# Wider products, split evictions: the first 56 tiles of the stage of u

## The chip, the cores and the metric

The kernel runs on one core of one Trainium2 chip. The metric is the device time of one execution in microseconds (us); 1671.91 us is the median of 3 runs of the kernel before (1670.87 to 1672.17). Engines are named as the profile names them: PE (TensorE matmuls) with PEld (its weight loads), DVE (VectorE), ACT (ScalarE), POOL (GpSimd) and SP, which only issues transfers here.

## The reference, cut to what matters

The program is three blocks over 256 tokens of width 1024: two attention and MLP layers, one layer with a state-space and an attention branch, and a mixture of 16,384 experts. The change is in the last one:

```python
def peer_ffn(x, w_q, sub_k1, sub_k2, u_tab, v_tab):
    q = x @ w_q                              # 8 heads, two halves of 128
    v1, i1 = top_k(q1 @ sub_k1.T, 16); v2, i2 = top_k(q2 @ sub_k2.T, 16)
    top_s, pos = top_k(v1[:, None] + v2[None, :], 16)
    experts, gates = i1 * 128 + i2 at pos, softmax(top_s)
    u = u_tab[experts]
    act = gelu(sum(u * x)) * gates
    return sum(act * v_tab[experts])
```

The kernel computes, for 224 of the 256 tokens, gelu(u_tab x) for all experts as one dense product (the stage of u), multiplies it by a dense table of gates that is zero for experts not chosen, and multiplies by v_tab (the stage of v). The other 32 tokens gather their rows.

## The kernel before, in words

The kernel is written by hand with a fixed order of instructions on each engine. `peer` starts on line 1537.

**The stage of u.** u_tab comes in 128 tiles of 128 experts, each 128x1024 words (8 blocks of 128x128). A `Weights` object streams them: SP loads a tile into one of four `raw` buffers, ACT copies it to `whi` (line 94, a rounded high part), and DVE or POOL subtracts to get `wlo` (line 96, the low part). There are 3 buffers of each part here, and a call of `take` splits tiles up to two ahead of the one it hands out. While `w.share` is 2 (the takes of tiles 0 to 47) every second split's subtraction goes to POOL: the even tiles of u go to DVE, the odd ones to POOL.

The tokens' side, `hT`, is split too, into `hTl` and `hTh`, two tiles of 128 x 8 x 256. Each tile of u takes 24 products of 224 columns (`mm_cols`, lines 156 and 159): 8 of whi with hTh, 8 of whi with hTl and 8 of wlo with hTh, all into the same 224 columns of a PSUM bank. `u_pair` (line 1762) gives two tiles one bank of the pool `side`, and one activation of 448 columns (line 1772) takes both out of PSUM through Gelu into S0.

**What DVE does beside it.** The routing (top 16 of the keys, then of the candidates, then the choice of indices) is a list of small jobs, `work`. `some` (line 1821) takes jobs up to a budget, and is called twice for each pair. The order on DVE for a pair is then: the subtraction of an even tile, two helpings of jobs, the next even tile's subtraction.

**What sets the order of evictions.** `w.post` keeps a function until the next `take`, which first issues its loads and splits and then flushes what was posted. So what is posted after tile i is issued behind the splits that the take of tile i+1 asks for. Pools hand out banks in rotation; `acc` has 4 and is free in this stage.

From pair U0 = 56 on (and for tiles 64 to 127) `u_pair` stays as it is.

Of the kernel before, what the change touches and what calls it, by code (L numbers as in the profile page):

```python
# [10 lines left out]
FT = mybir.dt.float32  # L11
FR = mybir.dt.float32r
# [3 lines left out]
AF = mybir.ActivationFunctionType  # L16
OP = mybir.AluOpType
AX = mybir.AxisListType

D = 1024  # L20
S = 256
# [7 lines left out]
UT, SE, U0, I0, YN, YA = 32, 19.5, 6, 10, 27.5, 29  # L29
# [108 lines left out]
class Net:  # L138
# [113 lines left out]
                after(hi, lo, pv)  # L252

    def new_T(self, pool, name):
        return tuple(pool.tile([128, 8, S], FR, name=name + x) for x in "hl")


    def sincos(self, ang, out, pool):
# [1274 lines left out]
    def peer(self, ctx, w, hT):  # L1533
        tc, nc, a = self.tc, self.nc, self.a
        V, G = nc.vector, nc.gpsimd
# [5 lines left out]
        N, GR = S - NS, 128 // NS  # L1541
        S0 = sp.tile([128, 64, N], FT, name="S0")
# [4 lines left out]

        eid = sp.tile([128, NS], I32, name="eid")
        eidf, gs, dots = (sp.tile([128, NS], FT, name=n) for n in ("eidf", "gs", "dots"))
        hTd = tuple(x[:, :, 0:N] for x in hT)  # L1550
        late = {}
        it = sp.tile([128, 128], FT, name="it")
        nc.gpsimd.dma_start(out=it, in_=a["iota"])
# [38 lines left out]
        def q_mm(i):  # L1592

            ps = self.acc.tile([128, 512], FT, name="acc")
            for hf in range(2):
                self.mm_cols(ps[:, 256 * hf:256 * hf + 256], w.next(), hT)
            return ps

        def q_T(i):

            w.flush()
            ps = self.bank()
            for hf in range(2):
                for t in range(2):
                    n = 2 * i + hf
                    nc.tensor.transpose(ps[:, 256 * hf + 128 * t:256 * hf + 128 * t + 128], qn[:, t, 128 * n:128 * n + 128],
                                        self.ident)
            return ps
# [91 lines left out]
        def dot_step(n):  # L1700

            fetch(a["un"], n)
            if 2 <= n < NS + 2:
                r = fetched.popleft()
                V.scalar_tensor_tensor(r, r, 1.0, xs, op0=OP.mult, op1=OP.mult, accum_out=dots[:, n - 2:n - 1])  # L1705
            if n == NS + 1:
                nc.scalar.activation(dots, dots, AF.Gelu_apprx_tanh)
                V.tensor_tensor(dots, dots, gs, op=OP.mult)
                late["sum"] = sp.tile([128, D], FT, name="xs")

        def sum_step(n):

            fetch(vn, n)
            if 2 <= n < NS + 2:
                r, y, m = fetched.popleft(), late["sum"], dots[:, n - 2:n - 1]
                if n == 2:
                    V.tensor_scalar(y, r, m, None, op0=OP.mult)
                else:
                    V.scalar_tensor_tensor(y, r, m, y, op0=OP.mult, op1=OP.add)
            if n == NS + 1:  # L1720
                for h in range(2):
                    ps = self.bank()
                    nc.tensor.matmul(ps, late["picks"], late["sum"][:, 512 * h:512 * h + 512], start=True, stop=True)
                    x = late["xr"][128 - NS:128, 1, 512 * h:512 * h + 512]
                    w.post(V.tensor_tensor, x, ps[128 - NS:128], x, op=OP.add)
# [22 lines left out]
        def gate_mm(hf, q):  # L1748
# [9 lines left out]
            if q % 2:  # L1758
                v = (late["S1"] if hf else S0)[:, :, 4 * q - 4:4 * q + 4]
                w.post(lambda: V.tensor_tensor(v, v, ps.rearrange("p (t c) -> p c t", c=64), op=OP.mult))  # L1760

        def u_pair(c, between=None):
            ps = self.bank()
            for x in range(2):
                wt = w.next()
                if x and between:
                    between()
                self.mm_cols(ps[:, 256 * x:256 * x + N], wt, hTd)
            if c == 64:
                late["S1"] = sp.tile([128, 64, N], FT, name="S1")  # L1770
            dst = S0[:, c:c + 2] if c < 64 else late["S1"][:, c - 64:c - 62]
            w.post(lambda: nc.scalar.activation(dst, ps.rearrange("p (a b) -> p a b", a=2)[:, :, 0:N], AF.Gelu_apprx_tanh))  # L1772
# [4 lines left out]
        for n, i in enumerate(order):  # L1777
            ps = q_T(i) if i < 2 else q_mm(i)
# [29 lines left out]
        def some(budget=16):  # L1808
            while work and budget >= work[0][1] // 2:
                f, n = work.popleft()  # L1810
                f()
                budget -= n

        def gate_step(q):

            if q >= 0 and q % 4 == 0:
                for i in range(q, q + 4):
                    gate_mm(i // NQ, i % NQ)
            if q + 4 < 2 * NQ:
                gate_gen((q + 4) // NQ, (q + 4) % NQ)  # L1820

        ops = deque()
        NQ, U0, V0 = N // 4, 56, 52
        for c in range(0, 64, 2):
            w.share = 2 if c < 48 else 0
            if c >= 60:
                gate_step(c - 64)
            u_pair(c, some)
            some()
            if c >= U0:  # L1830
                dot_step((c - U0) // 2)
# [3 lines left out]
        def gate_steps(n, end):  # L1835
            nonlocal q
            for _ in range(n):
                if q < end:
                    gate_step(q)
                    q += 2  # L1840

        def a_split(c, dst=None):
            src = S0[:, c] if c < 64 else late["S1"][:, c - 64]
            A = dst or sp.tile([128, 2 * N], FR, name="ahl", bufs=2)
            ah, al = A[:, 0:N], A[:, N:2 * N]
            nc.scalar.activation(ah, src, AF.Copy)  # L1846
            G.tensor_tensor(al, src, ah.bitcast(FT), op=OP.subtract)  # L1847
            return A

        for c in range(64, 128, 2):  # L1850
            w.share = 6
            if c == 126:
                w.share = 0
                A = []
                u_pair(c, lambda: (gate_steps(1, NQ), A.append(a_split(0))))
                w.flush()
            else:
                u_pair(c, lambda: gate_steps(1, NQ))
            dot_step((c - U0) // 2)
# [7 lines left out]
        acc = [self.acc.tile([128, 512], FT, name="acc") for _ in range(6)]  # L1867
        column = lambda k: acc[k][:, 0:N] if k < 4 else acc[2 + k // 2][:, 256 * (k % 2):256 * (k % 2) + N]

        def v_mm(c, A, wts, ks, last=False):  # L1870

            mm = nc.tensor.matmul
            parts = [(k, i, slice(128 * k, 128 * k + 128)) for k in ks for i in range(len(A))]
            for k, i, s in parts:
                first = c == 0 and i == 0
                if k < 4:
                    mm(acc[k][:, 0:2 * N], wts[i][0][:, s], A[i], start=first, stop=False)  # L1877
                else:
                    mm(column(k), wts[i][0][:, s], A[i][:, 0:N], start=first and k % 2 == 0, stop=False)  # L1879
            for k, i, s in parts:  # L1880
                if k >= 4:
                    mm(column(k), wts[i][0][:, s], A[i][:, N:2 * N], start=False, stop=False)  # L1882
            for k, i, s in parts:
                mm(column(k), wts[i][1][:, s], A[i][:, 0:N], start=False, stop=last and i == len(A) - 1 and (k < 4 or k % 2 == 1))  # L1884

        nxt = A.pop()
        for c in range(124):
            if c == 122:

                w.parts = Room(sp.tile([128, 64 * N], FR, name="S0"))  # L1890
            A = nxt
            wt = w.next()
            nxt = a_split(c + 1)
            v_mm(c, [A], [wt], range(8))
            if c % 2 == (c > 30):
                gate_steps(1, 2 * NQ)
            if c == 8:
                xr = late["xr"] = self.hTp.tile([128, 2, D], FT, name="hTh")
                gb = self.hTp.tile([128, D], FT, name="hTl")
                src = a["norm_f_g"]  # L1900
                nc.scalar.dma_start(out=gb, in_=bass.AP(tensor=src.tensor, offset=src.offset, ap=[[0, 128], [1, D]]))
                for t in range(2):
                    nc.scalar.dma_start(out=xr[:, t], in_=self.xd[t])
                late["picks"] = sp.tile([128, 128], FT, name="it")
                nc.scalar.dma_start(out=late["picks"], in_=a["sums"])
            if c >= V0 and c % 2 == 0:
                sum_step((c - V0) // 2)
# [29 lines left out]
        for b in range(4):  # L1937
# [3 lines left out]
            for i, k in enumerate(ks):  # L1941
                dst = oT[k // 4][:, k % 4]
# [14 lines left out]
        for t in range(2):  # L1957
            for h in range(2):
                c = slice(512 * h, 512 * h + 512)
                x = xr[:, t, c]  # L1960
# [212 lines left out]
```

## Time and profile before

| | before |
|---|---|
| median of 3 runs | 1671.91 us (1670.87 to 1672.17) |
| profiled execution | 1672.08 us, span 1670.0 us |
| PE busy | 1616.1 us (97%), 12410 matmuls |
| DVE busy | 1299.8 us (78%) |
| ACT busy | 845.9 us (51%) |
| POOL busy | 699.0 us (42%) |
| first matmul of the stage of u | 927.16 us into the span |
| first matmul of its tile 56 | 1083.38 us into the span |

The shares of busy time are averages over the whole program; the change touches only the 156 us between the last two rows. A matmul's duration in the profile overlaps with its neighbours, so its cost in a stream is read from the distance between starts.

### The profile page before, as it was taken

What the parts mean: (1) busy time and instruction counts of PE and PEld (TensorE: products, weight loads), DVE (VectorE), ACT (ScalarE), POOL (GpSimd) and SP (SyncE); (2) the same over time, 40 slices, a digit from 0 to 9 for tenths busy, and PEclk for the clock granted to TensorE, in tenths of its full rate; (3) what the DMA queues carried; (4) which work ended last, traced back from release to release, by engine and by line L of the source; (5) the groups of instructions that cost most, each with busy time, mean ns of one, the idle gap of its engine ahead of it and who ended that gap; (6) DMA issues with size and microseconds to landing.
All of it is one profiled execution on the core that took longest, in us unless ns stands there. A gap on an engine that the chain in (4) does not pass through costs nothing.

```text
span 1670.0 us, 31715 instructions
## 1 busy us (share of the span) xinstructions
PE 1616.1 (97%) x12410; PEld 1476.5 (88%) x12410; DVE 1299.8 (78%) x2318; ACT 845.9 (51%) x1308; POOL 699.0 (42%) x610
## 2 busy tenths in 40 slices
PE   8999999889999999997999999999999999999996
PEld 6788999767889998775879999999999999999996
DVE  6775997666769866787663899889999889877775
ACT  6555655455556454643445545544444444455553
POOL 2313529322148933673020454323343222277773
PEclk9999999989999999998999999999999999999998
DMA  7435565464356557823356455777777655689982
GB/s 248 143 122 169 166 188 177 165 205 131 107 187 195 184 162 252 305 77 126 101 171 217 159 177 194 247 228 262 254 258 251 207 178 181 195 291 302 305 301 77
DMA packets 94325, 328.49 MB, mean 197 GB/s; under 512 B 11920, under 2 KB 16176, under 8 KB 93280
## 3 DMA queue, kind: packets, MB, share of 16 engines
q1 hardware_dynamic: 82992, 285.27, 51.1%
q0 software_dynamic: 10176, 39.03, 7.4%
q10 hardware_dynamic: 1008, 2.17, 0.4%
q8 instruction: 97, 1.59, 0.4%
q14 instruction: 52, 0.43, 0.1%
HBM read 318.57 MB, written 7.47 MB: 195 GB/s over the span
## 4 chain that ended last, share of the span: by engine, by line
PE 82%; DVE 8%; ACT 3%; DMA 3%; issue 2%; POOL 1%; ACTq 0%; SPq 0%; POOLq 0%; DVEq 0%
PE side L159 19%; PE acc L159 15%; PE side L156 10%; PE acc L156 8%; PE acc L1884 7%; PE acc L1877 6%; PE acc L1882 3%; PE acc L1879 3%; DVE wlo L96 3%; DMA raw<-in_ws 3%; PE side L1757 2%; ACT whi L94 1%; PE side L399 1%; PE side L376 1%; PE side L375 1%
## 5 line engine op out<-in xcount | busy, mean ns | idle before, releaser
L96 DVE TENSOR_TENSOR wlo<-raw,whi 128x1024 fp32r<-128x1024 f32 x462 | 609.2, 1330 | 221.0 <-ACT whi L94 220.3
L94 ACT ACTIVATE whi<-raw 128x1024 fp32r<-128x1024 f32 x511 | 535.8, 1057 | 456.1 <-PE acc L1882 174.0
L159 PE MATMUL side<-hTh,wlo 128*128 128x224 f32 (+1 forms) x1664 | 224.4, 277 | 2.8 <-DVE wlo L96 2.5
L156 PE MATMUL side<-hTh,whi 128*128 128x224 f32 (+1 forms) x1664 | 225.5, 278 | 0.8 <-ACT Bst L108 0.8
L159 PE MATMUL side<-hTl,whi 128*128 128x224 f32 (+1 forms) x1664 | 223.6, 277 | 0.0
L156 PEld LDWEIGHTS side<-hTh,whi 128*128 128x128 f32 x1664 | 207.6, 191 | 4.0 <-ACT Bst L108 1.1
L159 PEld LDWEIGHTS side<-hTh,wlo 128*128 128x128 f32 x1664 | 205.7, 191 | 3.9 <-DVE wlo L96 3.3
L159 PEld LDWEIGHTS side<-hTl,whi 128*128 128x128 f32 x1664 | 205.9, 191 | 0.0
L96 POOL TENSOR_TENSOR wlo<-raw,whi 128x1024 fp32r<-128x1024 f32 x49 | 125.9, 2572 | 178.2 <-ACT whi L94 170.9
L1847 POOL TENSOR_TENSOR ahl<-S,ahl 128x224 fp32r<-128x224 f32 x125 | 123.4, 988 | 173.8 <-ACT ahl L1846 173.2
L1884 PE MATMUL acc<-ahl,wlo 128*128 128x224 f32 x992 | 130.9, 274 | 0.0
L156 PE MATMUL acc<-whi,hTh 128*128 128x512 f32 x384 | 124.2, 416 | 1.3 <-ACT whi L94 1.3
L1877 PE MATMUL acc<-ahl,whi 128*128 128x448 f32 x496 | 124.4, 372 | 0.7 <-ACT S L1772 0.7
L1884 PEld LDWEIGHTS acc<-ahl,wlo 128*128 128x128 f32 x992 | 120.7, 192 | 0.0
L159 PE MATMUL acc<-wlo,hTh 128*128 128x512 f32 x384 | 117.9, 400 | 1.2 <-DVE wlo L96 1.1
L159 PE MATMUL acc<-whi,hTl 128*128 128x512 f32 x384 | 117.9, 399 | 0.3 <-DVE hTl L222 0.3
L159 PEld LDWEIGHTS acc<-wlo,hTh 128*128 128x128 f32 x384 | 72.7, 190 | 20.7 <-DVE wlo L96 3.2
L797 POOL TENSOR_TENSOR th<-th,cv 128x256 f32<-128x256 f32 x44 | 47.6, 1082 | 103.0 <-DVE th L796 99.6
L783 DVE SCALAR_TENSOR_TENSOR cv<-side,cw,cv 128x254 f32<-128x254 f32 (+1 forms) x176 | 72.5, 472 | 22.3 <-ACT cv L780 22.3
L159 PEld LDWEIGHTS acc<-whi,hTl 128*128 128x128 f32 x384 | 72.9, 190 | 18.3 <-DVE hTl L222 0.8
L1877 PEld LDWEIGHTS acc<-ahl,whi 128*128 128x128 f32 x496 | 84.3, 190 | 5.2 <-issue 1.4
L1696 POOL DMA_INDIRECT rows<-in_un,eid x32 | 47.0, 1470 | 96.4 <-DVE rows L1705 94.3
(487 smaller groups left out, 2787.7 us busy)
## 6 DMA issues: line engine op xcount, KB each, us to landing
raw<-in_ws SPq DMA_DIRECT2D x259, 512.0 KB, 4.0
raw<-in_us SPq DMA_DIRECT2D x128, 512.0 KB, 3.9
raw<-in_vs SPq DMA_DIRECT2D x128, 512.0 KB, 4.2
dBst<-Bst SPq DMA_DIRECT2D x1, 2048.0 KB, 7.4
dCT<-CT SPq DMA_DIRECT2D x2, 1024.0 KB, 7.9
tg<-dBst POOLq DMA_DIRECT2D x1, 2048.0 KB, 9.4
gb<-in_g_ffn SPq DMA_DIRECT2D x2, 512.0 KB, 5.3
s5bc<-in_s5bc SPq DMA_DIRECT2D x2, 512.0 KB, 5.8
```

The costliest lines, as they stand in the source:

```text
L94: self.nc.scalar.activation(hi, t, AF.Copy)
L96: eng.tensor_tensor(lo, t, hi.bitcast(FT), op=OP.subtract)
L156: mm(ps, sh, mh, start=first, stop=False)
L159: mm(ps, sl if side == "s" else sh, ml if side == "m" else mh, start=False, stop=last and side == late)
L783: nc.vector.scalar_tensor_tensor(o[which][:, n:], p[which][:, :S - n], cw[which][:, 2 - n:3 - n], o[which][:, n:], op0=OP.mult, op1=OP.add)
L797: nc.gpsimd.tensor_tensor(th, th, o[1], op=OP.mult)
L1696: G.indirect_dma_start(out=r, out_offset=None, in_=table, in_offset=bass.IndirectOffsetOnAxis(ap=eid[:, n:n + 1], axis=0))
L1847: G.tensor_tensor(al, src, ah.bitcast(FT), op=OP.subtract)
L1877: mm(acc[k][:, 0:2 * N], wts[i][0][:, s], A[i], start=first, stop=False)
L1879: mm(column(k), wts[i][0][:, s], A[i][:, 0:N], start=first and k % 2 == 0, stop=False)
L1882: mm(column(k), wts[i][0][:, s], A[i][:, N:2 * N], start=False, stop=False)
L1884: mm(column(k), wts[i][1][:, s], A[i][:, 0:N], start=False, stop=last and i == len(A) - 1 and (k < 4 or k % 2 == 1))
```

## The change

For pairs below U0 the kernel calls `u_apart` in place of `u_pair`. `hTh` and `hTl` become the two halves of one tile, so that whi is multiplied by both at once: 8 products of 448 columns into columns 0 to 447 of a bank, then 8 of wlo with the high half into columns 0 to 223. Each tile of u has a bank of its own in `acc`. Then ACT copies columns 224 to 447 to S0 (one take later), DVE adds columns 0 to 223 to it (another take later), and after both tiles of a pair ACT applies Gelu in S0 (one more take later).

```diff
     def new_T(self, pool, name):
-        return tuple(pool.tile([128, 8, S], FR, name=name + x) for x in "hl")
+        self.pair = pool.tile([128, 2, 8, S], FR, name=name)
+        return self.pair[:, 0], self.pair[:, 1]
...
-        hTd = tuple(x[:, :, 0:N] for x in hT)
+        hTd = self.pair[:, 0, :, 0:N], self.pair[:, 1, :, 0:N]
...
+        def u_sum(ps, dst):
+            nc.scalar.activation(dst, ps[:, N:2 * N], AF.Copy)
+            w.post(V.tensor_tensor, dst, ps[:, 0:N], dst, op=OP.add)
+
+        def u_apart(c):
+            dst = S0[:, c:c + 2]
+            for x in range(2):
+                wt = w.next()
+                if x:
+                    some()
+                ps = self.acc.tile([128, 512], FT, name="acc")
+                for k in range(8):
+                    nc.tensor.matmul(ps[:, 0:2 * N], wt[0][:, 128 * k:128 * k + 128], self.pair[:, :, k, 0:N], start=k == 0,
+                                     stop=False)
+                for k in range(8):
+                    nc.tensor.matmul(ps[:, 0:N], wt[1][:, 128 * k:128 * k + 128], hTd[0][:, k], start=False, stop=k == 7)
+                w.post(u_sum, ps, dst[:, x])
+            w.post(w.post, w.post, nc.scalar.activation, dst, dst, AF.Gelu_apprx_tanh)
...
-            u_pair(c, some)
+            if c < U0:
+                u_apart(c)
+            else:
+                u_pair(c, some)
```

The rest of the diff reuses the joint tile's room in the stage of v.

On PE, tiles 4 and 5 of u, with the semaphores that an instruction waits for. Before (`side` is the bank of the pair):

```order
L156 MATMUL side<-hTh,whi 128x224 [waits Activation_49]
L156 MATMUL side<-hTh,whi 128x224 x7
L159 MATMUL side<-hTl,whi 128x224 x8
L159 MATMUL side<-hTh,wlo 128x224 [waits DVE_49]
L159 MATMUL side<-hTh,wlo 128x224 x7
L156 MATMUL side<-hTh,whi 128x224 [waits Activation_49]
L156 MATMUL side<-hTh,whi 128x224 x7
L159 MATMUL side<-hTl,whi 128x224 x8
L159 MATMUL side<-hTh,wlo 128x224 [waits Pool_49]
L159 MATMUL side<-hTh,wlo 128x224 x7
```

The same two tiles now, each in a bank of `acc`:

```order
L1777 MATMUL acc<-hT,whi 128x448 [waits DVE_49,Activation_49]
L1777 MATMUL acc<-hT,whi 128x448 x7
L1780 MATMUL acc<-hT,wlo 128x224 x8
L1777 MATMUL acc<-hT,whi 128x448 [waits DVE_49,Activation_49]
L1777 MATMUL acc<-hT,whi 128x448 x7
L1780 MATMUL acc<-hT,wlo 128x224 [waits Pool_49]
L1780 MATMUL acc<-hT,wlo 128x224 x7
```

The wait for DVE has moved from the 17th product of the even tile to its first, and the odd tile's first product has one too.

On DVE, from the subtraction for tile 4 of u to that for tile 6 (L1519 to L1529 are one routing job and the next, MAX and its followers). Before:

```order
L96 TENSOR_TENSOR wlo<-raw,whi 128x1024
L1519 MAX S_9262<-S_9262 128x8 x2
L1521 MAX_INDEX S_9262<-S_9262 128x8 x2
L1523 MATCH_REPLACE S_9262<-S_9262 128x128 x2
L1527 MAX S_9262<-S_9262 128x8 x2
L1529 MAX_INDEX S_9262<-S_9262 128x8 x2
```

The same place now (S_9252 is S0; L108 is where a posted function is called):

```order
L96 TENSOR_TENSOR wlo<-raw,whi 128x1024
L108 TENSOR_TENSOR S_9252<-acc,S_9252 128x224 x2
L1520 MAX S_9253<-S_9253 128x8 x2
L1522 MAX_INDEX S_9253<-S_9253 128x8 x2
L1524 MATCH_REPLACE S_9253<-S_9253 128x128 x2
L1528 MAX S_9253<-S_9253 128x8 x2
L1530 MAX_INDEX S_9253<-S_9253 128x8 x2
```

Two additions stand behind each subtraction for an even tile; the first is that of the tile four before it.

## Rows read from the trace of the kernel before

**Rows 1.** Windows: stretch, length, busy PE, PEld, DVE, ACT, POOL; PEclk; DMA

```profile
928.10:978.50 50.40, 50.21 (x449) 50.03 (x449) 50.37 (x266) 25.54 (x30) 27.66 (x11) 1.00 0.49 168
978.50:1031.00 52.50, 50.10 (x442) 49.42 (x442) 51.34 (x154) 26.07 (x32) 25.82 (x10) 1.00 0.56 183
1031.00:1059.50 28.50, 27.48 (x245) 27.09 (x244) 27.37 (x33) 16.50 (x22) 12.63 (x5) 1.00 0.66 218
1059.50:1083.50 24.00, 24.00 (x218) 24.00 (x217) 19.35 (x20) 12.70 (x18) 7.01 (x4) 1.00 0.78 264
```

**Rows 2.** Chain of waits, 976 to 1054 us, shares by line

```profile
by line: DVE wlo L96 31.8%; issue 8.6%; DVE S L1521 8.1%; DVE S L1529 8.1%; DVE S L1523 7.6%; DVE S L1527 7.2%; DVE S L1519 6.7%; DVE S L1666 6.2%; DVE S L1624 4.3%; DVE S L1658 3.1%; PE side L159 1.5%; ACT whi L94 1.4%; DVE S L1649 1.1%; D
```

**Rows 3.** Timeline of PE: start, duration, line, tiles, shape, count [idle before <-releaser]

```profile
985.36 1.16 PE L159 MATMUL side<-hTh,wlo 128*128 128x224 f32 x8 [2.06 <-DVE wlo L96]
986.35 1.06 PE L156 MATMUL side<-hTh,whi 128*128 128x224 f32 x8
989.03 1.06 PE L156 MATMUL side<-hTh,whi 128*128 128x224 f32 x8
...
1304.82 0.99 PE L1877 MATMUL acc<-ahl,whi 128*128 128x448 f32 x4
1305.65 0.60 PE L1879 MATMUL acc<-ahl,whi 128*128 128x224 f32 x4
1307.43 0.99 PE L1877 MATMUL acc<-ahl,whi 128*128 128x448 f32 x4
```

**Rows 4.** Timeline of DVE: subtractions for even tiles

```profile
928.13 1.23 DVE L96 TENSOR_TENSOR wlo<-raw,whi 128x1024 fp32r<-128x1024 f32 x1 [4.75 <-ACT whi L94]
933.96 1.21 DVE L96 TENSOR_TENSOR wlo<-raw,whi 128x1024 fp32r<-128x1024 f32 x1
...
976.41 1.21 DVE L96 TENSOR_TENSOR wlo<-raw,whi 128x1024 fp32r<-128x1024 f32 x1
984.10 1.21 DVE L96 TENSOR_TENSOR wlo<-raw,whi 128x1024 fp32r<-128x1024 f32 x1
1004.90 1.23 DVE L96 TENSOR_TENSOR wlo<-raw,whi 128x1024 fp32r<-128x1024 f32 x1
1009.73 1.50 DVE L96 TENSOR_TENSOR wlo<-raw,whi 128x1024 fp32r<-128x1024 f32 x1
1028.05 1.22 DVE L96 TENSOR_TENSOR wlo<-raw,whi 128x1024 fp32r<-128x1024 f32 x1
1059.47 1.22 DVE L96 TENSOR_TENSOR wlo<-raw,whi 128x1024 fp32r<-128x1024 f32 x1
```

**Rows 5.** Groups of the last 30 us, and timeline around 651 us

```profile
L1948 DVE TENSOR_TENSOR rows<-acc,rows 128x224 f32<-128x224 f32 x4 | 1.6, 391 | 1.7 <-ACT rows L1944 1.7
L1944 ACT ACTIVATE rows<-acc 128x224 f32<-128x224 f32 x4 | 1.4, 357 | 9.8 <-DVE rows L1946 7.4 <-PE acc L1884 2.5
...
650.61 1.47 POOL L804 TENSOR_TENSOR gl<-th,gh 128x256 fp32r<-128x256 f32 x1 [5.73 <-ACT gh L803]
651.48 1.66 DVE L783 SCALAR_TENSOR_TENSOR cv<-side,cw,cv 128x255 f32<-128x255 f32 x4
```

**Rows 6.** Timeline, 960 to 970 us: one tile, and the split after it

```profile
964.76 1.05 PE L156 MATMUL side<-hTh,whi 128*128 128x224 f32 x8
965.65 1.05 PE L159 MATMUL side<-hTl,whi 128*128 128x224 f32 x8
966.54 1.05 PE L159 MATMUL side<-hTh,wlo 128*128 128x224 f32 x8
966.74 1.06 ACT L94 ACTIVATE whi<-raw 128x1024 fp32r<-128x1024 f32 x1 [1.14 <-PE side L159]
967.88 2.40 POOL L96 TENSOR_TENSOR wlo<-raw,whi 128x1024 fp32r<-128x1024 f32 x1 [2.95 <-ACT whi L94]
```

**Rows 7.** Timeline around 1015 us: DVE beside POOL

```profile
1014.73 2.40 POOL L96 TENSOR_TENSOR wlo<-raw,whi 128x1024 fp32r<-128x1024 f32 x1 [1.24 <-ACT whi L94]
1014.83 3.37 DVE L96 TENSOR_TENSOR wlo<-raw,whi 128x1024 fp32r<-128x1024 f32 x1
1018.13 0.74 DVE L1519 MAX8 S<-S 128x8 f32<-128x256 f32 x2
```

More of the change, by code (lines that the diff above doesn't have):

```diff
@@ L1897, in peer @@
             if c == 8:
-                xr = late["xr"] = self.hTp.tile([128, 2, D], FT, name="hTh")
-                gb = self.hTp.tile([128, D], FT, name="hTl")
+                room = self.hTp.tile([128, 4, D], FT, name="hT")
+                xr, gb = room[:, 0:2], room[:, 2]
+                late["xr"] = xr
                 src = a["norm_f_g"]
```

## The prediction, made before the result was known

> **What bounds the kernel now.** PE is busy for 97% of the span, so a change that shortens PE's work looks like a gain. That is an average, and the stretch of the change has to be read by itself. First the windows [rows 1]: of the first 50.4 us of the stage of u DVE is busy for 50.37, of the next 52.5 for 51.34, of the next 28.5 for 27.37. Only in the last 24 us has it room (19.35). PE is busy for 50.1 of the second window's 52.5 us, so both are nearly full. Then the chain of waits [rows 2], which decides between two full engines: from 976 to 1054 us it runs along DVE's subtractions (31.8%) and its routing jobs, with PE's products at 1.5%. PE itself shows what it waits for: 2.06 us before a product with wlo, released by DVE [rows 3]. Before 976 us PE still lives on tiles that were split ahead.
>
> DVE's step from one even tile's subtraction to the next, one pair of tiles, is 5.83 us in the first part (928.13 to 933.96) and 4.83 in the second (1004.90 to 1009.73) [rows 4]. PE's is 2 x 2.68 = 5.36 us (986.35 to 989.03 for one tile of 24 products, 111.7 ns each) [rows 3]. The three parts below have 8, 9 and 6 pairs, counted from the subtractions at 928.13, 976.41, 1028.05 and 1059.47 [rows 4]; the pairs left run to 1083.4.
>
> **What PE saves.** In the stage of v four products of 448 columns take 0.83 us (1304.82 to 1305.65), 207.5 ns each [rows 3]. A tile of u becomes 8 x 207.5 + 8 x 111.7 ns = 2.55 us in place of 2.68, the pair 5.11. The tile of v, by the same two prices, would be 4 x 207.5 + 16 x 111.7 = 2.62 us, and is 2.61 (1304.82 to 1307.43). Over 56 tiles that is 7.2 us, if PE set the pace throughout.
>
> The Trainium skill, "TensorE: Matmul & The Clock Gate", section "Back-to-back issue gap", gives N/2.4 + 2.5 ns between warm products. By that a joined product would save only 2.5 ns, and the change 448 x 2.5 ns = 1.1 us. The rows show 223.4 ns for two narrow products against 207.5 for the wide one, so the sum goes by the rows.
>
> **What DVE gets.** 56 additions of 128x224, one operand in PSUM. The nearest row is the addition of the same shape at the end of the program, 391 ns alone [rows 5]. In a row, an instruction starts a little before the one ahead ends: the job at 1018.13 by 0.07 us, for the subtraction ahead of it ends at 1014.83 + 3.37 = 1018.20 [rows 7]. So the bounds are 0.32 and 0.39; I take 0.35. Four DVE operations with one operand in PSUM began while POOL still worked (650.61 to 652.08) and took 1.66 us, 0.41 each for 255 columns [rows 5]; that leaves no room for a wait, so I add nothing for POOL. A pair on DVE becomes 5.83 + 0.70 = 6.53 us in the first part and 4.83 + 0.70 = 5.53 in the second. Both are above PE's 5.11: what PE saves is not on the path, except at the end.
>
> ACT gets 56 copies at 357 ns [rows 5], 20 us, in a stretch where it is busy for half [rows 1]; its Gelu of 448 columns stays, with its input in SBUF. I cost both at nothing. What hides them is ACT's free time, 24.9 us over 8.6 pairs of 5.83, so 2.9 per pair against 0.71 of copies; without it the copy of whi queued behind would be late, and 0.71 us per pair would be the price. DMA is unchanged.
>
> **What the moved wait does.** The first product of a tile now needs its bank, which the addition of the tile four before frees, and on DVE that addition stands right behind the subtraction for the very tile that PE wants to begin. Before, PE could do 16 products (1.79 us) before it needed that subtraction. So PE starts each even tile later against DVE, and everything that PE's progress triggers shifts with it. One such thing is POOL's subtraction for the odd tile three ahead: PE's last product with whi frees the buffer, 0.20 us later ACT starts the copy, and 1.14 us after that POOL begins [rows 6].
>
> DVE's and POOL's subtractions do not run beside each other. At 1014.83 DVE's came 0.10 us behind POOL's 2.40 us, took 3.37 us, and its next operation began at 1018.13, 1.00 us after POOL's end [rows 7]. Measured from the moment that PE starts an even tile: last product with whi 1.66 us, + 0.20 + 1.14 = 3.00, POOL busy until 5.40. DVE, after the addition that released PE, has one more addition and two helpings of jobs, and is back at the next subtraction after 6.53 - 1.14 - 0.35 = 5.04 us in the first part and 4.0 in the second (1.14 is the subtraction's 1.21 less the overlap). Both fall inside POOL's 3.00 to 5.40. DVE then waits for 5.40, needs 1.00 for the rest, 0.39 for the addition and 0.05 until PE starts (as from 984.10 + 1.21 to 985.36 [rows 3, 4]): 6.84 us for a pair, in either part. The four engines would go round in a ring. In the old order the wait sits behind the last product with whi, so neither the 1.66 us nor the addition is in the ring: 0.20 + 1.14 + 2.40 + 1.07 (the subtraction's own end) + 0.05 = 4.86 us, under PE's 5.36.
>
> **The sum, on the profiled execution (1672.08 us; the median is 0.17 lower).**
> - First part, 48.3 us for 8 pairs, 1.7 us above 8 x 5.83 for stalls that I keep. Three pairs at 6.53 until PE's lead is gone, five at 6.84, + 1.7 = 55.5: +7.2. No ring: 8 x 6.53 + 1.7 = 53.9, +5.6.
> - Second part, 51.6 us for 9 pairs. One has a long stall and takes 7.69 us (976.41 to 984.10), now 8.4; the others 8 x 6.84: 63.1, +11.5. No ring: 8.4 + 8 x 5.53 = 52.6, +1.0.
> - Third part, 31.4 us for 6 pairs. DVE's jobs are shorter here, it reaches the subtraction some 2.8 us after PE's start, just before POOL would begin, and may pass first. Between 5.11 (PE alone) and 6.84 I take the middle, 5.98: 35.9, +4.5; ends -0.7 and +9.6.
> - The rest, 23.9 us. DVE's 19.35 us + 9 x 0.35 = 22.5, PE's 9 tiles x 2.55 = 23.0: between -0.9 and +1, I take 0.
>
> Together +23.2: 1695 us. Ends for this case: 1690 (third part at its low end) to 1702 (at its high end, additions at 0.39).
>
> **Rivals.**
> - *No ring, DVE's sum alone.* If the collisions stay as they are, the additions up to 1059.5 us (23.5 pairs x 0.70 = 16.5) less the DVE idle of that stretch (131.4 - 129.1 = 2.3) lengthen it by 14.2: 1686. For it: the collisions of today come and go (1.21 to 3.37 us [rows 4, 7]). Against: the ring holds itself in place, because PE starts as soon as it is released.
> - *No ring and no collisions.* +5.6 + 1.0 + 1.8 (third part at 5.53) = +8.4: 1680.5. It needs DVE to come to its subtraction first every time.
> - *PE decides after all (faster).* The additions fit beside PE's products and PE keeps the 7.2 us: 1665. Place: pairs of the first two parts. It decides where DVE's pair is under 5.11 us; at 5.83 and 4.83 before anything is added the second part would need additions under 0.14 us, against 0.32 at the least, and the first can't have it. Part of DVE's busy time is waiting for POOL, which speaks for a little slack.
> - *The joint tile costs elsewhere.* Layers that write hT could now wait for readers of either half. The instructions and their waits are the same outside the stage of u, so I price this at 0 and give it no chance of its own.
>
> **How the numbers follow.** Ring 0.55; DVE's sum 0.20; no collisions 0.13; still longer than 1703 (the ring in the third part as well, and the copies of ACT late) 0.05; PE decides 0.04; within 0.2% 0.03 (3.3 us, about what runs of this kernel tell from no change). The range that leaves out some 2 in 10 at both ends goes from just under the case without collisions to the ring's top: 1680 to 1703. Faster 0.04, same 0.03, slower 0.93.
>
> **What would show it.** Tile 56 starts some 180 us after tile 0 in place of 156. The additions take near 0.39 us each. PE's idle time before line 1777 is released by the addition (line 108 on DVE), 1.5 us or more per pair, and none is left before line 1780 for DVE. POOL's subtractions come every 6.8 us, and most of DVE's in the second part take over 2 us because POOL is in front. The stages of v and of the second half of u keep their lengths. I am wrong if DVE has idle time in the first 100 us of the stage, or if its subtractions keep 1.2 us there (then the no-collision case), or if PE shows no waits at line 1777.

## The result, and the profile after

The changed kernel takes 1692.84 us (median of 4 runs, 1689.07 to 1694.77) beside 1671.39 us for the kernel before: a ratio of 1.0127, 95% interval [1.0109, 1.0146]. The profiled execution took 1689.07 us, 17.0 more than the one of before. Two repeats on other chips gave 1.0124 and 1.0105 (below), so the loss is some 17 to 22 us.

It lies where the change is. From the first product of tile 0 to the first of tile 56 the stage takes 175.5 us (925.04 to 1100.55) in place of 156.2: +19.3. From there to the end there are 586.75 us in place of 586.6, and what stands ahead is 2.1 us shorter in this execution. The stage came out at 175.5 us in the profiles of both repeats too.

First the windows of the changed kernel over the four parts of [rows 1], cut at the same DVE subtractions (columns as there):

```profile
926.00:984.40 58.40, 48.51 (x283) 45.25 (x281) 58.40 (x274) 28.29 (x44) 26.06 (x10) 0.94 0.41 144
984.40:1042.70 58.30, 49.91 (x293) 46.63 (x291) 56.97 (x174) 31.76 (x49) 28.74 (x11) 0.94 0.48 163
1042.70:1077.30 34.60, 31.02 (x184) 29.11 (x185) 33.35 (x50) 20.89 (x35) 13.66 (x5) 0.95 0.53 182
1077.30:1100.60 23.30, 22.57 (x145) 21.26 (x144) 21.11 (x29) 15.29 (x27) 6.88 (x4) 1.00 0.72 253
```

The third number after the length is DVE: as full as before, in longer parts. PE, the first, was busy for 50.21 of 50.40 us and is now for 48.51 of 58.40. The granted clock is 0.94 or 0.95 in three parts, where it was 1.00.

The groups of the stage, up to the last of its additions and Gelus (line, engine, operation, count | busy us, mean ns | idle before and its releaser):

```profile
L1777 PE MATMUL acc<-hT,whi 128*128 128x448 f32 x448 | 106.1, 381 | 21.7 <-DVE S L108 21.7
L1764 ACT ACTIVATE S<-acc 128x224 f32<-128x224 f32 x56 | 19.2, 342 | 2.8 <-PE acc L1780 2.8
L108 DVE TENSOR_TENSOR S<-acc,S 128x224 f32<-128x224 f32 x56 | 19.5, 380 | 0.6 <-ACT S L1764 0.6
L108 ACT ACTIVATE S<-S 128x448 f32<-128x448 f32 x28 | 16.0, 572 | 20.1 <-DVE S L108 20.1
```

Over the stage PE waits 21.7 us before first products of tiles, in 10 waits, and ACT 20.1 us before its Gelus, both for additions. The additions take 380 ns each, and two in a row 0.68 us.

The chain of waits from 940 to 1090 us, shares by line, to be read beside [rows 2]:

```profile
by line: PE acc L1777 18.4%; DVE wlo L96 18.3%; PE acc L1780 9.7%; DVE S L1522 6.8%; DVE S L1524 6.5%; DVE S L108 6.1%; DVE S L1530 5.9%; DVE S L1520 5.2%; DVE S L1528 4.8%; issue 4.6%; DVE S L1625 4.3%; DVE S L1667 3.2%; DVE S L1659 2.7%; 
```

PE's products have a share now (28.1% for lines 1777 and 1780), and the additions 6.1%; the rest is still DVE's subtractions and routing jobs.

The ring of the prediction is there for two pairs in a row, at the end of the first part. Timeline (start, duration, engine, line, count, idle before with its releaser):

```profile
972.59 1.86 PE L1777 MATMUL acc<-hT,whi 128*128 128x448 f32 x8 [1.53 <-DVE S L108]
...
974.54 1.07 ACT L94 ACTIVATE whi<-raw 128x1024 fp32r<-128x1024 f32 x1 [0.94 <-ACT S L1764]
...
975.68 2.41 POOL L96 TENSOR_TENSOR wlo<-raw,whi 128x1024 fp32r<-128x1024 f32 x1 [4.62 <-ACT whi L94]
...
977.34 1.84 DVE L96 TENSOR_TENSOR wlo<-raw,whi 128x1024 fp32r<-128x1024 f32 x1
979.10 0.68 DVE L108 TENSOR_TENSOR S<-acc,S 128x224 f32<-128x224 f32 x2
979.62 1.86 PE L1777 MATMUL acc<-hT,whi 128*128 128x448 f32 x8 [1.76 <-DVE S L108]
...
984.37 1.84 DVE L96 TENSOR_TENSOR wlo<-raw,whi 128x1024 fp32r<-128x1024 f32 x1
```

PE starts at 972.59, POOL 3.09 us later, DVE meets POOL's subtraction and ends 1.09 us after it, the addition releases PE at 979.62: 7.03 us per pair. Further on the same engines go another way round:

```profile
998.68 1.21 DVE L96 TENSOR_TENSOR wlo<-raw,whi 128x1024 fp32r<-128x1024 f32 x1
999.81 0.68 DVE L108 TENSOR_TENSOR S<-acc,S 128x224 f32<-128x224 f32 x2
...
1001.64 1.80 PE L1777 MATMUL acc<-hT,whi 128*128 128x448 f32 x8
1003.28 1.05 PE L1780 MATMUL acc<-hT,wlo 128*128 128x224 f32 x8
...
1004.08 1.21 DVE L96 TENSOR_TENSOR wlo<-raw,whi 128x1024 fp32r<-128x1024 f32 x1
1004.16 1.80 PE L1777 MATMUL acc<-hT,whi 128*128 128x448 f32 x8
...
1009.49 1.21 DVE L96 TENSOR_TENSOR wlo<-raw,whi 128x1024 fp32r<-128x1024 f32 x1
```

Here DVE comes first, its subtraction keeps 1.21 us, a pair takes 5.40 us (998.68 to 1004.08), and PE runs without a wait: a tile in 2.52 us (1001.64 to 1004.16), a wide product in 205 ns (1.64 / 8) and a narrow one in 110.

### The profile page after: what moved, and what is told of

The parts are those of the page before. It is cut to its first block, busy times and chain, and to the rows that moved or that the text cites. A ratio compares the mean times of both kernels' runs of the same rounds, so it can differ in the third digit from the quotient of the medians.

```text
span 1687.3 us, 31003 instructions
## 1 busy us (share of the span) xinstructions
PE 1614.0 (96%) x11962; PEld 1466.8 (87%) x11962; DVE 1323.0 (78%) x2374; ACT 862.6 (51%) x1364; POOL 699.4 (41%) x610
## 4 chain that ended last, share of the span: by engine, by line
PE 81%; DVE 11%; ACT 3%; issue 2%; POOL 2%; DMA 2%; ACTq 0%; SPq 0%; POOLq 0%; DVEq 0%
PE acc L159 16%; PE side L159 16%; PE acc L156 8%; PE side L156 8%; PE acc L1909 7%; PE acc L1902 6%; PE acc L1907 3%; PE acc L1904 3%; DVE wlo L96 3%; PE side L1758 2%; PE acc L1777 2%; DMA raw<-in_ws 1%; ACT whi L94 1%; PE acc L1780 1%; DVE S L1522 1%
## 5 line engine op out<-in xcount | busy, mean ns | idle before, releaser
L156 PE MATMUL side<-hT,whi 128*128 128x256 f32 (+1 forms) x1216 | 166.1, 279 | 0.8 <-ACT Bst L108 0.8
L159 PE MATMUL side<-hT,wlo 128*128 128x256 f32 (+1 forms) x1216 | 164.6, 278 | 0.0
L159 PE MATMUL side<-hT,whi 128*128 128x256 f32 (+1 forms) x1216 | 164.4, 277 | 0.0
L156 PEld LDWEIGHTS side<-hT,whi 128*128 128x128 f32 x1216 | 153.0, 190 | 4.0 <-ACT Bst L108 1.1
L159 PEld LDWEIGHTS side<-hT,whi 128*128 128x128 f32 x1216 | 151.3, 190 | 0.0
L159 PEld LDWEIGHTS side<-hT,wlo 128*128 128x128 f32 x1216 | 151.1, 190 | 0.0
L1777 PE MATMUL acc<-hT,whi 128*128 128x448 f32 x448 | 106.1, 381 | 21.7 <-DVE S L108 21.7
L156 PE MATMUL acc<-whi,hT 128*128 128x512 f32 x384 | 124.2, 416 | 1.3 <-ACT whi L94 1.3
L159 PE MATMUL acc<-wlo,hT 128*128 128x512 f32 x384 | 117.9, 399 | 1.2 <-DVE wlo L96 1.1
L159 PE MATMUL acc<-whi,hT 128*128 128x512 f32 x384 | 117.7, 399 | 0.3 <-DVE hT L222 0.3
L1777 PEld LDWEIGHTS acc<-hT,whi 128*128 128x128 f32 x448 | 83.0, 196 | 29.1 <-issue 23.2
L159 PEld LDWEIGHTS acc<-wlo,hT 128*128 128x128 f32 x384 | 72.8, 190 | 20.4 <-DVE wlo L96 2.8
L159 PEld LDWEIGHTS acc<-whi,hT 128*128 128x128 f32 x384 | 72.9, 190 | 18.4 <-DVE hT L222 0.7
```

Of the source, the lines that this page charges most:

```text
L156: mm(ps, sh, mh, start=first, stop=False)
L159: mm(ps, sl if side == "s" else sh, ml if side == "m" else mh, start=False, stop=last and side == late)
L1777: nc.tensor.matmul(ps[:, 0:2 * N], wt[0][:, 128 * k:128 * k + 128], self.pair[:, :, k, 0:N], start=k == 0, stop=False)
```

## The experiments

Three theories. *DVE's sum*: the additions are work on an engine that was already full, and the stage is as long as what DVE has to do. *The ring*: the moved wait sets the pace, and the sum of work is second. *PE decides*: what PE does or waits for sets the stage, whatever DVE has. The repeats stand first, as a scale for the rest; each ratio is to runs of the kernel before on the same chip.

**The changed kernel again, twice.**

> The changed kernel again, unaltered, for a comparison on one chip with the others of this group and with the eight-bank kernel. If the moved wait has a price of its own, it stays at 1692 to 1694, some 4 us over the eight-bank kernel's ratio to before (1.0103); if that difference was chance, its ratio comes out at 1.010 to 1.011.

1689.20 us (1688.03 to 1696.74), ratio 1.0124 [1.0102, 1.0146].

> The changed kernel as it is, a third time, on the chip of g1_no_waits, so that the two can be set against each other. DVE's sum alone: 1686 to 1690 us, at most 2 us over g1. The moved wait as a term of its own: 3 to 6 us over g1.

1689.05 us (1687.93 to 1690.68), ratio 1.0105 [1.0090, 1.0119].

**The additions alone**, on the kernel before: its narrow products and its one Gelu stay, and DVE adds each tile's columns into a spare tile that nothing reads.

```diff
...
+            if c < U0:
+                for x in range(2):
+                    w.post(w.post, V.tensor_tensor, extra, ps[:, 256 * x:256 * x + N], extra, op=OP.add)
```

> The kernel before, with its 24 narrow products and its waits, and 56 additions of 128x224 (a PSUM operand, into a spare tile that nothing reads) at the same places on DVE as in the changed kernel. Theory of DVE's sum: 56 x 0.33 us less the 2 to 3 us that DVE was idle, 1686 to 1690. Ring theory: without the moved wait DVE's subtractions meet POOL's less often; about 1680 (first part 6.5 us a pair, second 5.5).

1687.63 us (1684.91 to 1690.87), ratio 1.0107 [1.0091, 1.0122]. No product is wide, no wait of a first product or of a Gelu in its trace ends with an addition, and a loss as large as the changed kernel's is there. Its stage in one window (columns as in [rows 1]):

```profile
923.90:1097.30 173.40, 158.94 (x1353) 156.63 (x1353) 166.72 (x522) 81.53 (x100) 71.43 (x29) 0.97 0.52 174
```

**The change without copies and additions.** ACT applies Gelu to columns 0 to 223 of each tile as soon as it can, so the new waits go as well.

```diff
-                w.post(u_sum, ps, dst[:, x])
-            w.post(w.post, w.post, nc.scalar.activation, dst, dst, AF.Gelu_apprx_tanh)
+                w.post(nc.scalar.activation, dst[:, x], ps[:, 0:N], AF.Gelu_apprx_tanh)
```

> The changed kernel without its copies and additions: Gelu is taken per tile from columns 0 to 223 of its bank, so that the products of whi with the low half of hT, in columns 224 to 447, are made but left out of the result. Both theories: DVE's list is that of the kernel before, so the stage is again near 156 us and the total 1666 to 1672; PE alone would save 7 us (1664), but DVE's 5.83 and 4.83 us a pair allow no more than some 3 of them. If the wide products themselves cost something that I have not seen, it is over 1675.

1671.70 us (1669.33 to 1675.04), ratio 1.0005 [0.9996, 1.0014]. The loss is gone, and PE's 448 wide products in place of 896 narrow ones bring nothing that can be seen: DVE has the same list of work as before. In its profiled execution (1673.47 us, above its median) the stage takes 159.5 us, with DVE busy for 153.02.

**Half of the additions**: for the even tile of a pair alone.

```diff
-        def u_sum(ps, dst):
-            nc.scalar.activation(dst, ps[:, N:2 * N], AF.Copy)
-            w.post(V.tensor_tensor, dst, ps[:, 0:N], dst, op=OP.add)
+        def u_sum(ps, dst, x):
+            nc.scalar.activation(dst, ps[:, 0:N] if x else ps[:, N:2 * N], AF.Copy)
+            if not x:
+                w.post(V.tensor_tensor, dst, ps[:, 0:N], dst, op=OP.add)
...
-                w.post(u_sum, ps, dst[:, x])
+                w.post(u_sum, ps, dst[:, x], x)
```

> The changed kernel with the addition made for the even tile of a pair only: 28 additions instead of 56; for the odd tile ACT copies columns 0 to 223 and the products of whi with the low half are left out of the result. Theory of DVE's sum: half the additions, half the loss, 1680 to 1683 (each addition 0.33 us, with DVE full throughout). Ring theory: the addition behind the subtraction that the even tile waits for is still there, so PE still starts even tiles late: 1687 or more.

1680.28 us (1678.29 to 1681.17), ratio 1.0052 [1.0038, 1.0066]: about half of the loss, though the wait for the even tile's addition is still there. The loss goes with the number of additions. Its stage in one window:

```profile
925.90:1091.70 165.80, 152.21 (x905) 141.07 (x905) 160.32 (x496) 95.53 (x154) 70.26 (x29) 0.95 0.54 183
```

**The wait on the banks taken away.** The odd tile's bank comes from the pool of four that `u_pair` used, so eight banks take turns and the addition in question is long done.

```diff
-                ps = self.acc.tile([128, 512], FT, name="acc")
+                ps = (self.side if x else self.acc).tile([128, 512], FT, name="side" if x else "acc")
```

> The changed kernel with one edit: the odd tile of a pair takes its bank from the pool side, the even one from acc, so that eight banks rotate and a tile's first product waits for the addition eight tiles before instead of four. All additions stay. Ring theory (the moved wait makes PE, ACT's copy, POOL's and DVE's subtraction go round): PE no longer waits for the addition behind the subtraction it needs; about 1680, stage of the first 56 tiles near 165 us, no idle before line 1777 released by DVE. Theory of DVE's sum (56 additions on an engine that is already full): nothing changes by 3 us, 1688 to 1694, stage 173 to 177 us; PE's waits only move from the first product to the first one with wlo.

1687.94 us (1687.03 to 1689.10), ratio 1.0103 [1.0087, 1.0118]: at the lower end of the three results for the changed kernel, and from none of them clearly apart; far from the 1680 that was expected of the ring. The waits of its stage (engine, line, what released it: total us, times, longest):

```profile
ACT S L108 <- DVE S L108: 34.3, 16, 5.8
PEld acc L1780 <- DVE wlo L96: 20.8, 12, 4.6
PE acc L1780 <- DVE wlo L96: 16.3, 12, 4.2
```

PE now waits where it did before the change, for DVE's subtraction, and ACT's wait before the Gelu has grown to 34.3 us, from 19.8 in the same stretch of the changed kernel.

**The Gelu's wait taken away**: the Gelu of a pair is posted two takes later, the banks stay four.

```diff
-            w.post(w.post, w.post, nc.scalar.activation, dst, dst, AF.Gelu_apprx_tanh)
+            w.post(w.post, w.post, w.post, w.post, nc.scalar.activation, dst, dst, AF.Gelu_apprx_tanh)
```

> The changed kernel with one edit: the Gelu of a pair is posted two takes later, as in g1_no_waits; the banks stay the changed kernel's four, so the wait for an addition ahead of a tile's first product stays. If what g1 won (6 us) is ACT's wait before the Gelu, which kept the copies of whi behind it, the ratio to before comes near g1's 1.007 (1682 to 1685 us). If it is the bank, it stays near the changed kernel's 1.0105 to 1.0127 (1688 to 1693 us). If both are needed, it lies between, 1685 to 1688 us.

1691.24 us (1687.42 to 1693.44), ratio 1.0113 [1.0096, 1.0130]: no gain. The waits of its stage:

```profile
ACT whi L94 <- PE acc L1777: 53.5, 29, 5.4
PE acc L1777 <- DVE S L108: 23.7, 11, 3.3
```

ACT, free of the one wait, waits for PE's products instead, and PE for the additions as in the changed kernel.

**Both waits taken away**: the last two edits together.

> As e1_banks (eight accumulators in turn, so the wait for an addition no longer stands ahead of a tile's first product), and the Gelu of a pair posted two takes later, so ACT doesn't wait for the pair's second addition either. Theory of DVE's sum: the 56 additions are work on a full engine and no wait of another engine decides; the time is that of e1, 1686 to 1689 us, and DVE stays busy in the first 100 us of the stage. Theory of the waits (what ACT lost, 20 us before its Gelus, delayed the copies of whi and with them everything): 1684 us or less.

1683.01 us (1681.92 to 1685.44), ratio 1.0070 [1.0057, 1.0083]; the changed kernel on the same chip has 1.0105 [1.0090, 1.0119]. So taking both away gave some 6 us, and taking away one gained nothing that shows. What was expected of DVE's sum alone (1686 to 1689, and at most 2 us between the two kernels) failed; "1684 or less" held.

One window over the stage shows where these microseconds are. In the kernel before, then the changed one, then the one without the two waits (columns as in [rows 1]):

```profile
927.20:1083.40 156.20, 152.60 (x1353) 151.34 (x1353) 148.42 (x469) 81.62 (x100) 73.13 (x29) 1.00 0.59 196
```

```profile
925.00:1100.60 175.60, 153.01 (x906) 143.19 (x905) 169.82 (x522) 97.24 (x155) 75.34 (x29) 0.95 0.50 172
```

```profile
926.70:1094.50 167.80, 150.72 (x906) 136.47 (x905) 162.03 (x523) 96.23 (x154) 71.56 (x29) 0.98 0.50 180
```

The stage less DVE's busy time is 7.8, 5.8 and 5.8 us. The stage is as long as DVE is busy and 6 to 8 us more, in all three; the additions alone (173.4 us, DVE 166.72) and half of them (165.8, 160.32) agree. But busy is not the same as work. DVE's subtractions, some casts and some other routing operations stretch when POOL works, and which ones meet it differs. Their groups in the changed kernel, then without the two waits:

```profile
L96 DVE TENSOR_TENSOR wlo<-raw,whi 128x1024 fp32r<-128x1024 f32 x32 | 48.3, 1510 | 6.4 <-ACT whi L94 6.2
L1663 DVE TENSOR_TENSOR S<-S 128x1024 bf16<-128x1024 bf16 x8 | 9.7, 1214 | 0.3
L1659 DVE TENSOR_TENSOR S<-S,itb 128x1024 bf16<-128x1024 bf16 x8 | 7.5, 932 | 0.1
L1625 DVE CAST S<-S 128x256 bf16<-128x256 uint32 x2 | 6.5, 3271 | 0.0
L1651 DVE TENSOR_SCALAR S<-S 128x128 uint32<-128x128 uint32 x2 | 2.7, 1327 | 0.0
```

```profile
L96 DVE TENSOR_TENSOR wlo<-raw,whi 128x1024 fp32r<-128x1024 f32 x32 | 49.9, 1561 | 6.4 <-ACT whi L94 6.2
L1663 DVE TENSOR_TENSOR S<-S 128x1024 bf16<-128x1024 bf16 x8 | 7.6, 954 | 0.3
L1659 DVE TENSOR_TENSOR S<-S,itb 128x1024 bf16<-128x1024 bf16 x8 | 5.8, 727 | 0.1
L1625 DVE CAST S<-S 128x256 bf16<-128x256 uint32 x2 | 3.6, 1822 | 0.0
L1651 DVE TENSOR_SCALAR S<-S 128x128 uint32<-128x128 uint32 x2 | 0.4, 220 | 0.0
```

The last four rows together are 26.4 us against 17.4: 9.0 us of stretch, less 1.6 in the subtractions, beside the 7.8 us by which DVE's busy times differ. Whether the two waits cause this meeting or the phases only fell well without them is open: the kernel with the additions alone has neither wait, and DVE is busy there for 4.7 us more than here. The meetings differ as much between kernels that have neither wait, as DVE's 32 subtractions show, first with the additions alone, then without copies and additions:

```profile
L96 DVE TENSOR_TENSOR wlo<-raw,whi 128x1024 fp32r<-128x1024 f32 x32 | 48.5, 1522 | 6.4 <-ACT whi L94 6.2
L96 DVE TENSOR_TENSOR wlo<-raw,whi 128x1024 fp32r<-128x1024 f32 x32 | 56.7, 1779 | 7.7 <-ACT whi L94 7.5
```

So the 6 us are shown as what this pair of edits gave, not as a price of the waits.

**Relief for DVE.** If DVE is the bound, giving its subtractions to POOL should free the stage. First all of them in the first 48 tiles (`share` 1 in place of 2), in the changed kernel:

```diff
-            w.share = 2 if c < 48 else 0
+            w.share = 1 if c < 48 else 0
```

> The changed kernel with every subtraction of the takes of tiles 0 to 47 on POOL, none on DVE. DVE loses 1.14 us per pair and gets 0.66 of additions. Theory of DVE's sum: DVE falls under the time of before in the first two parts (5.35 and 4.35 a pair), PE at 5.05 and POOL at 4.8 come next: 1666 to 1674. Ring theory: DVE has no subtraction to meet POOL's with, except its routing products of two SBUF operands; about the same, 1666 to 1676. If neither DVE nor its meetings with POOL were the cause, it stays over 1685.

1669.87 us (1667.88 to 1671.49), ratio 0.9990 [0.9981, 0.9999]. The loss is gone. POOL is busy for 129.8 of 156.1 us, and DVE's operation at line 1663 takes 2254 ns in the mean, in place of 1214 in the changed kernel. So next all of them only up to tile 33, then every second one:

```diff
+            w.share = 1 if c < 34 else 2 if c < 48 else 0
```

> The changed kernel with all subtractions of the takes of tiles 0 to 33 on POOL, and every second one from 34 to 47 as before (where DVE's routing products of two SBUF operands meet POOL's). Theory of DVE's sum: DVE is relieved of 1.14 us a pair for 17 pairs and PE's 5.05 or POOL's 4.8 set the pace there; 1663 to 1668, below the kernel before and below its narrow twin in this group by 2 to 5 us. If the wide products can't pay even with DVE relieved, it is at or over that twin.

1669.44 us (1666.92 to 1671.34), ratio 0.9989 [0.9980, 0.9998]: not the 1663 to 1668 that were expected of DVE's sum. Then the same line in the kernel before, with its narrow products:

> The kernel before (narrow products, no additions) with the same subtractions on POOL as the last one. DVE's pair falls to 4.7 and 3.7 us, so PE's 5.36 sets the pace in the first 17 pairs: the 6 us that PE waited in this stage go in part, 1665 to 1669. The difference to its wide twin is then what the wide products are worth when DVE isn't the bound: 17 x 0.31 = 5 us at most.

1666.17 us (1664.65 to 1667.72), ratio 0.9972 [0.9960, 0.9983]: 4.5 us under the kernel before, and under its wide twin, where the wide one had been expected 2 to 5 us faster. Its stage in one window:

```profile
927.50:1079.20 151.70, 151.30 (x1353) 150.91 (x1352) 131.82 (x427) 82.31 (x101) 112.12 (x46) 1.00 0.61 202
```

and its chain of waits from 927 to 1080 us, shares by line:

```profile
by line: PE side L159 64.4%; PE side L156 32.5%; POOL wlo L96 1.2%; DVE S L1666 0.8%; PE side L1615 0.5%; PE side L1671 0.5%; issue 0.1%; POOLq L96 0.0%
```

PE is busy throughout and DVE has 20 us to spare: now PE decides, for the first time in this stage. With the wide products PE has less to do, but its stage takes 154.8 us with PE at 146.72, and waits for additions (4.7 us) and for POOL (2.0) are among its gaps. Last, the wide products only for the first 24 tiles, where DVE has most relief (`if c < 24: u_apart(c)`):

> The schedule of subtractions of f3_narrow_pool (all on POOL for c below 34, every second to 48), the joined products only for c below 24 (12 pairs), the old order for the rest. If PE's saving pays once POOL has the subtractions, the 24 tiles give up to 24 x 0.13 = 3 us against f3: 1663 to 1665 us. If the 24 additions and the later wait cost as much as the products save, 1666 to 1669 us.

1667.05 us (1664.94 to 1677.62), ratio 0.9977 [0.9964, 0.9989]: not to be told from the narrow kernel's 0.9972; the 3 us that 24 shorter tiles could give don't show.

## Why the prediction was right

The time came out where it was predicted (1695.0, range 1680 to 1703), and the larger part of the reason held: DVE decides, and what PE saves is not on the path. The ring, which carried the number, kept its period for two pairs, and the number is in part luck: the first part came out 2.9 us above its term and the second 4.8 below.

- **DVE decides, and PE's saving is not on the path: right.** Taking away the additions and leaving the wide products gave back the loss and no more (1.0005); the additions alone made it (1.0107).
- **The prices: right.** A tile of 2.52 us (predicted 2.55), two additions in 0.68 us (0.70). By the Trainium skill ("TensorE: Matmul & The Clock Gate", "Back-to-back issue gap") a wide product would be 448 / 2.4 + 2.5 = 189 ns, as an estimate from the gap that it gives for an isolated product; the rows show 205 in a stream of products with a weight load each, and the rows decide. The additions at 999.81 ran beside POOL's subtraction and kept 0.68, as argued, though the row behind the argument was misread: four operations in 1.66 us from 651.48 are 0.41 apart, so only two of them began before POOL's end at 652.08.
- **The ring: seen, and given too many pairs.** Its period is 7.03 us (predicted 6.84), but only for the pairs that PE starts at 972.59 and 979.62. By parts, the measured lengths less those of before against the terms predicted: first +10.1 (58.37 - 48.28) against +7.2, second +6.7 (58.30 - 51.64) against +11.5, third +3.2 (34.65 - 31.42) against +4.5, the rest -0.7 against 0. Together +19.3 against +23.2. The step that failed is the second part's: "both fall inside POOL's 3.00 to 5.40". The ring does not hold itself in place. From 998.68 DVE comes first for a while, and five of this part's nine pairs take 5.40 to 5.68 us, near the 5.53 without a ring; the three longest, 7.50 to 8.91, hold a cast of 3.36, a subtraction of 3.30 and a TENSOR_SCALAR (line 1651) of 2.44 us, each behind POOL. What let DVE come first the runs do not isolate; the trace has a candidate, told with the clock below.
- **Most of DVE's subtractions over 2 us in the second part: wrong.** One of its nine was (3.30 us at 1021.30). All 32 of the stage together took 48.3 us, against 49.9 before. What met POOL more than before were other operations of DVE: two on two SBUF operands (lines 1659 and 1663), a cast (1625) and a TENSOR_SCALAR (1651), which have one.
- **No ring, DVE's sum (the rival at 1686): nearer than I gave it credit for.** Half of the additions cost half, which a ring held by the even tile's addition would not do, and without both waits the kernel is at 1683.0, between the two rivals without a ring (1680.5 and 1686). Taking the moved wait and ACT's wait away gave 6 us, not the 9 between 1686 and 1695, and how much of it belongs to the waits is open.
- **ACT at nothing: wrong in kind.** Its copies fit in its free time, as costed, but the Gelu holds the copies of whi queued behind it for 20.1 us, and I had priced no wait on ACT. Taken away alone it gave nothing (1.0113); both together gave the 6 us.
- **The clock: no term at all.** Lowered, it made two pairs of the first part 1.4 us longer each (last section).

What would have shown it wrong: DVE has little idle time in the first 100 us (58.40 of 58.40, 56.97 of 58.30), and PE's waits at line 1777 are there, though 10 for 28 pairs and not one for each. The third sign, subtractions that keep 1.2 us, came half true: 9 of the 15 in the first 100 us kept it.

## What to carry to other kernels

Before a change moves work from one engine to another, read who is full in that stage: here 448 products were saved on an engine that was waiting, and paid for with 56 additions on the engine that it waited for. Of two waits that stand side by side, taking away either showed nothing and taking away both gave 6 us, so test them together before calling them free, and before giving them the gain see what else moved: here it was how often DVE met POOL. The gain in this stage lay in a single line that moves DVE's work to an engine with room.

## What the runs showed of the hardware

**The first of two engines keeps its pace, and the second pays.** With POOL ahead, DVE's subtraction takes 1.84 us in place of 1.21 (977.34). With DVE ahead, POOL's takes longer, as these rows of the changed kernel show, and so does a cast on DVE behind a POOL operation:

```profile
987.28 3.69 POOL L1627 TENSOR_TENSOR S<-S 128x2048 f32<-128x2048 f32 x1 [2.15 <-DVE S L1528]
987.76 3.36 DVE L1625 CAST S<-S 128x256 bf16<-128x256 uint32 x1
...
999.41 2.74 POOL L96 TENSOR_TENSOR wlo<-raw,whi 128x1024 fp32r<-128x1024 f32 x1 [6.05 <-PE acc L1780]
1004.66 2.90 POOL L96 TENSOR_TENSOR wlo<-raw,whi 128x1024 fp32r<-128x1024 f32 x1 [2.51 <-ACT whi L94]
```

POOL's subtraction takes 2.40 us alone, and here 2.74 and 2.90, with DVE's subtractions begun 0.73 and 0.58 us ahead of it; the cast ends 0.15 us after POOL. The Trainium skill, "SBUF — State Buffer", section "Who interferes with whom", says that the order of issue decides which of the two blocks, and that an instruction of DVE with at most one SBUF input does not contend, outside the modes that use both ports, which `cast` and `tensor_scalar` can enter. The rows agree with the order. They agree with the rest as far as they go: the additions, with their other operand in PSUM, kept 380 ns, and the 64 index searches over 128 columns took 17.3 us together (17.4 before), while the cast, with one SBUF input, stretched. In which mode it ran no run shows.

**The clock fell after some waits.** In the kernel before, the granted clock is 1.00 throughout this stage. In the changed one it falls in five stretches, each behind a wait of PE. The first in the timeline, with what came of it:

```profile
947.20 2.70 PE L1777 MATMUL acc<-hT,whi 128*128 128x448 f32 x8 [1.74 <-DVE S L108]
949.70 1.84 PE L1780 MATMUL acc<-hT,wlo 128*128 128x224 f32 x8
951.38 1.80 PE L1777 MATMUL acc<-hT,whi 128*128 128x448 f32 x8
951.68 2.40 POOL L96 TENSOR_TENSOR wlo<-raw,whi 128x1024 fp32r<-128x1024 f32 x1 [6.01 <-PE acc L1780]
951.96 3.20 DVE L96 TENSOR_TENSOR wlo<-raw,whi 128x1024 fp32r<-128x1024 f32 x1
955.61 1.87 PE L1777 MATMUL acc<-hT,whi 128*128 128x448 f32 x8 [1.54 <-DVE S L108]
```

and windows of it and of the ring's pair, which begins with a wait of 1.53 us:

```profile
947.00:951.50 4.50, 4.30 (x17) 4.06 (x18) 4.50 (x31) 1.88 (x3) 0.00 (x0) 0.62 0.62 237
972.00:979.00 7.00, 5.27 (x32) 4.87 (x32) 7.00 (x36) 3.19 (x5) 2.41 (x1) 1.00 0.43 152
```

The tile at 947.20 takes 4.18 us in place of 2.52, its narrow products 210 ns in place of 110: near the lower level, 1.2 GHz, for most of it. The tiles behind waits of 1.53 and 1.76 us (972.59, 979.62) ran at 1.00, and so did one behind 2.33 us (1044.34). What tells them apart the runs don't show.

Part of the loss is on the path. PE's slow products free POOL's buffer late: POOL begins 4.48 us after PE's start (947.20 to 951.68), where it is 3.09 in the ring, DVE ends behind it, and PE starts again after 8.41 us in place of 7.03. The stretch at 964.20 repeats it (POOL at 968.66, PE at 972.59: 4.46 and 8.39). In the third, at 994.93, POOL begins at 999.41, again 4.48 us later, and there DVE had come first at 998.68; 3.09 us would have put POOL ahead of it, at 998.02. So the lower clock may be what opened the ring; no run here tests that.
